# A GLA layer and an S5 layer in one kernel: the S5 kernel products finished a step later, drained by ScalarE, and read as Toeplitz blocks straight from the kernel table

## The chip, the cores and the metric

One core of one Trainium2 chip. The metric is the device time of one execution in microseconds (us); lower is better. Line numbers (L1335) are those of the kernel before, and times from the trace count from the start of its span.

## What is computed

Two layers of a decoder trunk over 512 tokens of width 1024. Layer 0 is chunked gated linear attention (GLA, four heads), layer 1 a state-space mixer (S5) with 128 groups of 16 channels and 64 complex states. Each mixer has a gate path and a residual, and a norm follows. The part that the change touches prepares the S5 layer:

```python
lam_bar = jnp.exp(lam * dt)
b_bar = ((lam_bar - 1.0) / lam)[..., None] * b_cplx
bu = lax.complex(einsum('blgi,gpi->blgp', u32, real(b_bar)),
                 einsum('blgi,gpi->blgp', u32, imag(b_bar)))
_, states = lax.associative_scan(combine, (a, bu), axis=1)
y = einsum('blgp,gip->blgi', real(states), c_re) - einsum('blgp,gip->blgi', imag(states), c_im)
y = gelu(y + d_skip * u32)
y = y * sigmoid(y @ w_glu + b_glu) * silu(z)
```

The kernel does the scan in chunks of T = 8 steps. For each group it needs a 16 x 16 response for every lag within a chunk ("the kernel", C lam_bar^t B, with d_skip at lag 0), laid out as a Toeplitz block of 128 rows (8 steps x 16 channels), and two factors that carry the state in and out of a chunk ("B" and "C" below). All depend on the parameters alone, so they are worked out while layer 0 runs.

## The kernel before, in words

**Layer 0.** For each head, four dense products (proj_v, proj_qk, proj_z, proj_out) run on TensorE (PE). Every factor is split into a high and a low part, and one product is three matmuls (`three`, L201 to L203 or L205 to L207). `wunit` (L176 to L197) brings a weight unit of 512 KB into `wraw` (two buffers) and splits it into two tiles of the ring `whl` (8 tiles before the change). In one form of it ScalarE (ACT) writes the high half (L185) and the negated high half (L186), and a GpSimd (POOL) DMA then adds the weights to the latter in place (L187). In the others VectorE (DVE) or POOL subtracts (L162, L165). Between the products stands the attention itself: scores (L494, L496, masked by DVE L498), their split (L170, L171), the states (L516, L173, L174), and the sum over heads into the residual `xx` (L542).

**The preparation of S5** is the class `S5Prep`, woven into layer 0. There are 16 batches (cb) of 8 groups. `plan` lists steps, and `hook`, called as the dense products advance, takes one whenever a counter that grows by RATES reaches 1. LOWS sets how far a step's priority is lowered, and a step's instructions are held behind the last instruction issued on each engine then. A list scheduler with its own model of durations then fixes the order on every engine. For one batch:

- Step F(cb): `finish_b(cb-1)` adds two halves of the C factor on DVE (`z += z2`, L1325) and stores the B factor to `bmd` (`store`: ACT cast L1319, DVE difference L1320, DMA L1321 on SyncE's queue, SP). `compute(cb)` works on POOL (L1295 to L1313) and leaves bo, z, z2 and bh. `load(cb+1)` issues four loads on SP (L1278, L1280, L1283, L1284). The last, `pp<-pw`, has a single buffer, which `compute` reads at L1304.
- Step Z(cb): `finish_z(cb-1)` stores z to `cmd`, then makes the **kernel product**: four matmuls in fp32 (L1335, eight records each time) of bh and z into one PSUM bank `pt`. ACT drains the even half with a scale (L1339), and DVE reads the odd half from PSUM, scales it and adds the even one in a single instruction (L1341). POOL adds the d_skip term and makes the fp16 pair (L1345 to L1347), and SP stores it to the kernel table `kz` (L1348). Then `gcopy(cb-2)` (L1353) copies, from DRAM to DRAM, the rows of `kz` into full Toeplitz blocks `gmd` (512 KB a batch).

**Layer 1** loads for every batch, by `loadw` (L568 to L584), `bmd`, `tab`, `gmd` and `cmd`, then runs the state products and the scan of the chunks, and after that the w_glu and s_wout products. The loads from `gmd` are six of 256 KB (batches 0 to 2, two each, into `big` tiles) and 13 of 512 KB (into `q` tiles of the ring Q4, 9 tiles).

Of the kernel before, what the change touches and what calls it, by code (L numbers as in the profile page):

```python
# [11 lines left out]
F16 = mybir.dt.float16  # L12
I32 = mybir.dt.int32
U8 = mybir.dt.uint8
AF = mybir.ActivationFunctionType
# [4 lines left out]
MUL, ADD, SUB = ALU.mult, ALU.add, ALU.subtract  # L20

P = 128
# [9 lines left out]
T = 8  # L32
NC = SEQ // T
GB = 8
NB = 16
KW = 15 * 16
# [12 lines left out]
SU = 11  # L49
SS = 22  # L50
SE = 3
WR, WH, Q4, BIG = 2, 8, 9, 28
TOFF = 5
SMALL = [0, 1, 3, 4, 5]
NPRE = 3
# [6 lines left out]
SEQ0 = 'h0 u h2 u h4 u s h6 u x0 t x1 q0 q1 t'  # L62
GP = 4
RATES = [0.84, 0.84, 0.88, 0.94, 0.94]
LOWS = {'F': 0, 'Z': 20, 'E': 100, 'G': 0}
ETABS = [2, 3, 3, 3, 3, 3, 3, 3, 4, 4, 4, 4, 4, 4, 4, 7, 8]
POS = [[0, 0, 1, 2, 1, 2, 3, 1, 2, 3, 3], [0, 1, 1, 3, 4, 5, 6, 5, 5, 7, 9], [0, 1, 3, 4, 4, 5, 6, 5, 6, 8, 8], [1,
    1, 4, 4, 4, 5, 6, 6, 6, 6, 8], [0, 0, 0, 0]]
# [22 lines left out]
def trunk_kernel(  # L91
# [6 lines left out]
    V, A, G, S, PE = nc.vector, nc.scalar, nc.gpsimd, nc.sync, nc.tensor  # L98
    sb = ctx.enter_context(tc.tile_pool(name="sb", bufs=1))
    ps = ctx.enter_context(tc.tile_pool(name="ps", bufs=1, space=PSUM))  # L100
    dr = ctx.enter_context(tc.tile_pool(name="dr", bufs=1, space=DRAM))
    cnt = [0]

    def T_(shape, tag, bufs, dt=F32):
        cnt[0] += 1
        return sb.tile(shape, dt, tag=tag, name=f"{tag}_{cnt[0]}", bufs=bufs)
# [20 lines left out]
    def q4(dt=F32, n=1024):  # L127
        return T_([P, n], "q4", Q4, dt)
# [207 lines left out]
    prep = S5Prep(tc, dr, C_, T_, PT, ident, q4, q2, big, tmp, s_bi, s_xc)  # L336
# [4 lines left out]
    @contextmanager  # L341
    def later(n):
        tc.cur_priority += n
        yield
        tc.cur_priority -= n
# [13 lines left out]
    plan = []  # L359
    ne = 0  # L360
    for cb in range(NB + 1):
# [3 lines left out]
        while ne < ETABS[cb]:  # L365
            plan.append(("E", ne))
            ne += 1
    plan.append(("G", NB - 1))
    pace = [0.0]
    phase = [0]  # L370

    def hook():
        pace[0] += RATES[phase[0]]
        while pace[0] >= 1:
            pace[0] -= 1
            if plan:
                st = plan.pop(0)
                with later(LOWS[st[0]]):
                    prep.step(mark, *st)
# [187 lines left out]

    def loadw(cb, src, dt=F16):  # L568
        n = 1024 if dt == F16 else 512
        if src is prep.gmd:  # L570
            srcs = [src[cb, 4 * k:4 * k + 4].rearrange("g p w -> p g w") for k in range(2)]
            full = src[cb].rearrange("g p w -> p g w")
        else:
            srcs = [src[cb][:, k * n:(k + 1) * n] for k in range(2)]
            full = src[cb]
        fit = (lambda t: t.rearrange("p (g w) -> p g w", w=2 * P)) if src is prep.gmd else (lambda t: t)
        if cb < NPRE:
            w = [T_([P, n], "big", BIG, dt) for _ in range(2)]
            for k in range(2):
                S.dma_start(out=fit(w[k]), in_=srcs[k])  # L580
            return w
        t = q4(dt, 2 * n)
        S.dma_start(out=fit(t), in_=full)
        return [t[:, :n], t[:, n:]]  # L584

    def wsel(w):
        return [[w[k][:, g * P:(g + 1) * P] for g in range(GB)] for k in range(2)]
# [1 line left out]
    def gsel(w):  # L589
        v = [t.rearrange("p (g q k) -> p k g q", k=2, g=GB // 2) for t in w]  # L590
        return [[v[g // 4][:, k, g % 4] for g in range(GB)] for k in range(2)]
# [5 lines left out]

    def load_b(cb):
        t = st_[cb]
        t["gh"] = gsel(loadw(cb, prep.gmd))  # L600
        t["cm"] = wsel(loadw(cb, prep.cmd))

    v0 = ([], [])
# [35 lines left out]
    for h in range(NH):  # L639
# [22 lines left out]
        z = proj_z(h, box)  # L662
# [230 lines left out]
    w = win()  # L893
# [22 lines left out]
    for tb in range(NT):  # L916
        for k in range(2):
            S.dma_start(out=f(x1p)[k * 64:(k + 1) * 64, 2 * tb:2 * tb + 2].rearrange("p q d -> p (q d)"),
                        in_=x1d.rearrange("(c j) d -> j c d", j=T)[2 * tb + k])
# [21 lines left out]
class S5Prep:  # L941
    def __init__(self, tc, dr, C_, T_, PT, ident, q4, q2, big, tmp, s_bi, s_xc):
        self.tc = tc
        self.nc = nc = tc.nc
        self.C_, self.T_, self.PT, self.ident = C_, T_, PT, ident
        self.q4, self.q2, self.big, self.tmp = q4, q2, big, tmp
        self.s_bi, self.s_xc = s_bi, s_xc
        self.kz = dr.tile([NG, 16, KW * 2], F16, name="kz")
        self.bmd = dr.tile([NB, P, 2 * GB * P], F16, name="bmd")
        self.cmd = dr.tile([NB, P, 2 * GB * P], F16, name="cmd")  # L950
        self.gmd = dr.tile([NB, GB, P, 2 * P], F16, name="gmd")
        self.tab = dr.tile([NB, P, 2 * GB * NC], F32, name="tab")
        self.pw = dr.tile([2 * NS, NG, 2 * T], F32, name="pw")
        self.lpt = dr.tile([T, NG, 2, NS], F32, name="lpt")
        self.bcd = dr.tile([2, NS, NG], F32, name="bcd")
        self.r8d = dr.tile([NS, NG], F32, name="r8d")
        self.kdd = dr.tile([NG, 16], F32, name="kdd")
        self.etd = dr.tile([NG], F32, name="etd")
        self.t = 0
        self.ld = {}  # L960
        self.res = {}
# [325 lines left out]
    def compute(self, cb):  # L1287
        G = self.nc.gpsimd
        tt = G.tensor_tensor
        lp, bb, xc, pp = self.ld.pop(cb)  # L1290
        gs = slice(cb * GB, (cb + 1) * GB)
        v = lambda t: t.rearrange("p (g r q) -> p g r q", g=GB, r=2)
        bo, m = self.q4(), self.q4()
        lp4, bb4, bo4, m4 = v(lp), v(bb), v(bo), v(m)
        tt(out=m, in0=lp, in1=bb, op=MUL)  # L1295
        tt(out=bo4[:, :, 0], in0=m4[:, :, 0], in1=m4[:, :, 1], op=SUB)
        tt(out=m4[:, :, 0], in0=lp4[:, :, 0], in1=bb4[:, :, 1], op=MUL)
        tt(out=m4[:, :, 1], in0=lp4[:, :, 1], in1=bb4[:, :, 0], op=MUL)  # L1298
        tt(out=bo4[:, :, 1], in0=m4[:, :, 0], in1=m4[:, :, 1], op=ADD)
        x4 = xc.rearrange("p (g k i) -> p g k i", g=GB, k=4)  # L1300
        z, z2 = self.q4(), m
        sh = [P, GB, T, 16]
        w4 = lambda t: t.rearrange("p (g t i) -> p g t i", g=GB, t=T)
        tt(out=w4(z), in0=x4[:, :, 0].unsqueeze(2).to_broadcast(sh),  # L1304
           in1=pp[:, :, 0:T].unsqueeze(3).to_broadcast(sh), op=MUL)
        tt(out=w4(z2), in0=x4[:, :, 1].unsqueeze(2).to_broadcast(sh),
           in1=pp[:, :, T:].unsqueeze(3).to_broadcast(sh), op=MUL)
        bh = self.C2([P, GB, 16], "bh")
        b2 = self.C2([P, GB, 16], "bh2")
        s3 = [P, GB, 16]  # L1310
        tt(out=bh, in0=x4[:, :, 2], in1=self.BA[:, gs].unsqueeze(2).to_broadcast(s3), op=MUL)
        tt(out=b2, in0=x4[:, :, 3], in1=self.BB[:, gs].unsqueeze(2).to_broadcast(s3), op=MUL)
        tt(out=bh, in0=bh, in1=b2, op=ADD)  # L1313
        self.res[cb] = (bo, z, z2, bh)
# [10 lines left out]
        self.nc.vector.tensor_tensor(out=z, in0=z, in1=z2, op=ADD)  # L1325
        self.store(bo, self.bmd[cb])

    def finish_z(self, cb):
        nc = self.nc
        V, A, PE, S = nc.vector, nc.scalar, nc.tensor, nc.sync  # L1330
        bo, z, z2, bh = self.res.pop(cb)
        self.store(z, self.cmd[cb])
        pk = self.PT()
        for q in range(4):
            PE.matmul(pk[32 * q:32 * q + 32, 0:2 * P],  # L1335
                      lhsT=bh[:, 2 * q:2 * q + 2, :].rearrange("p a b -> p (a b)"),
                      rhs=z[:, 2 * q * P:(2 * q + 2) * P], start=True, stop=True, tile_position=(0, 32 * q))
        ke = self.tmp()[:, :P]
        A.activation(out=ke, in_=pk[:, 0:P], func=AF.Copy, scale=self.par[:, 0:1])  # L1339
        kf = self.C2([P, P, 2], "kf", F16)  # L1340
        V.scalar_tensor_tensor(out=ke, in0=pk[:, P:2 * P], scalar=self.par[:, 1:2], in1=ke, op0=MUL, op1=ADD)  # L1341
        G = nc.gpsimd
        dk = self.C2([P, 16], "dk")
        G.tensor_tensor(out=dk, in0=self.dm, in1=self.kd[:, cb:cb + 1].to_broadcast([P, 16]), op=MUL)
        G.tensor_tensor(out=ke[:, 0:16], in0=ke[:, 0:16], in1=dk, op=ADD)  # L1345
        G.tensor_copy(out=kf[:, :, 0], in_=ke)
        G.tensor_tensor(out=kf[:, :, 1], in0=ke, in1=kf[:, :, 0], op=SUB)  # L1347
        S.dma_start(out=self.kz[cb * GB:(cb + 1) * GB, :, 224:480].rearrange("g i w -> (g i) w"),  # L1348
                    in_=kf.rearrange("p w k -> p (w k)"))

    def gcopy(self, cb):
        src = bass.AP(self.kz.tensor, self.kz[cb * GB].offset + 7 * 32, [[2 * KW, P], [-32, T], [1, 2 * P]])
        self.nc.sync.dma_start(out=self.gmd[cb].rearrange("g (i j) w -> (g i) j w", j=T), in_=src)  # L1353

    def step(self, mark, code, cb):
        with ExitStack() as st:
            for k in ("pe", "act", "dve", "sp"):
                st.enter_context(self.tc.issue_after(mark[k]))
            if code == "F":
                if cb:  # L1360
                    self.finish_b(cb - 1)
                else:
                    self.load(0)
                if cb < NB:
                    self.compute(cb)
                if cb + 1 < NB:
                    self.load(cb + 1)
            elif code == "Z":
                self.finish_z(cb - 1)
                if cb >= 2:  # L1370
                    self.gcopy(cb - 2)
            elif code == "G":
                self.gcopy(cb)
            else:
                self.etab(cb)

# [55 lines left out]
```

## Time and profile before

| | |
|---|---|
| median of 3 runs | 1060.6 us (1058.78 to 1062.19) |
| the profiled execution | 1062.0 us, span 1060.3 us |
| mean granted clock of TensorE | 0.939 of full speed |
| busy time in the span: PE, DVE, POOL, ACT | 935.8, 723.4, 511.7, 465.0 us |
| share of the 16 DMA engines: SP queue, POOL queue | 54.7%, 9.9% |
| read from and written to HBM | 167.7 MB, 45.6 MB |

An engine's busy time is the time in which it worked on an instruction; for PE the ends of matmuls are modelled. The clock column of a view (PEclk) is the share of 2.4 GHz that TensorE was granted. "X <- Y" in a view of waits says that X started when Y ended, by the semaphores in the trace.

### The profile page before, as it was taken

To read this page: it belongs to the slowest core of one execution; us is meant where nothing else is said; L and a number is where in the kernel's file an instruction comes from. 1 tells how busy PE (TensorE), PEld (TensorE's weight loads), DVE (VectorE), ACT (ScalarE), POOL (GpSimd) and SP (SyncE) were. 2 spreads that over 40 slices of the span, in tenths; PEclk is the share of its full clock that TensorE was granted. 3 is DMA by queue.
4 is the path that set the end of the run, shared out by engine and by line. 5 is a ranking of instruction groups with operands and counts; after the bars stand their busy time and mean duration, and the time that the engine had idled before them with its cause. 6 is when DMAs were issued, how large, how long until landed. Compare 5 with 4: busy or idle time off the path is not lost. (4 is left out here: it accounts for less than half of the span.)

```text
span 1060.3 us, 13642 instructions
## 1 busy us (share of the span) xinstructions
PE 935.8 (88%) x5019; PEld 728.6 (69%) x5019; DVE 723.4 (68%) x884; ACT 465.0 (44%) x675; POOL 511.7 (48%) x477
## 2 busy tenths in 40 slices
PE   6895976897779798679979999999998999999996
PEld 5573754575556676557867777777777888888885
DVE  5793569948998889989634778799987432424322
ACT  5553333535445535343545783743453432313222
POOL 4174709877887969898963334353314000000000
PEclk9897987899979898899979999999998999999998
DMA  8884466899779898999578447697864332253312
GB/s 259 225 177 93 88 172 194 249 299 256 224 217 249 223 292 267 238 289 313 197 233 254 142 134 238 200 301 249 266 198 119 113 97 100 93 165 100 100 60 79
DMA packets 118706, 205.78 MB, mean 194 GB/s; under 512 B 32400, under 2 KB 69824, under 8 KB 118640
## 3 DMA queue, kind: packets, MB, share of 16 engines
q1 hardware_dynamic: 110208, 180.90, 54.7%
q0 software_dynamic: 5472, 19.02, 9.9%
q10 hardware_dynamic: 2960, 4.99, 1.3%
q8 instruction: 39, 0.64, 0.2%
q14 instruction: 27, 0.22, 0.1%
HBM read 167.69 MB, written 45.59 MB: 201 GB/s over the span
## 5 line engine op out<-in xcount | busy, mean ns | idle before, releaser
L205 PE MATMUL pd<-whl,actA 128*128 128x512 f32 x384 | 155.7, 414 | 21.6 <-ACT whl L161 9.3
L162 DVE TENSOR_TENSOR whl<-wraw,whl 128x1024 fp32r<-128x1024 f32 x61 | 76.2, 1249 | 144.4 <-ACT whl L161 144.3
L161 ACT CAST whl<-wraw 128x1024 fp32r<-128x1024 f32 x84 | 88.0, 1048 | 166.6 <-PE pt L202 45.7
L206 PE MATMUL pd<-whl,actA 128*128 128x512 f32 x384 | 157.1, 409 | 0.0
L207 PE MATMUL pd<-whl,actA 128*128 128x512 f32 x384 | 156.4, 408 | 0.0
L273 POOL TENSOR_TENSOR rstd<-rv,neghalf 128x1 f32<-128x1 f32 (+1 forms) x6 | 4.3, 716 | 247.1 <-DVE rv L272 247.1
L205 PEld LDWEIGHTS pd<-whl,actA 128*128 128x128 f32 x384 | 75.5, 197 | 42.5 <-ACT whl L161 9.3
L201 PE MATMUL pd<-actA,whl 128*128 128x512 f32 x256 | 101.6, 403 | 3.2 <-ACT u L734 3.2
L203 PE MATMUL pd<-actA,whl 128*128 128x512 f32 x256 | 101.3, 396 | 0.0
L205 PE MATMUL pd<-whl,q 128*128 128x512 f32 x192 | 80.9, 423 | 8.5 <-DVE big L165 3.2
L206 PEld LDWEIGHTS pd<-whl,actA 128*128 128x128 f32 x384 | 75.5, 197 | 17.4 <-issue 1.2
L207 PEld LDWEIGHTS pd<-whl,actA 128*128 128x128 f32 x384 | 75.2, 196 | 17.3 <-issue 1.2
L162 POOL TENSOR_TENSOR whl<-wraw,whl 128x1024 fp32r<-128x1024 f32 x23 | 57.3, 2492 | 52.6 <-ACT whl L161 49.2
L206 PE MATMUL pd<-whl,q 128*128 128x512 f32 x192 | 79.9, 417 | 0.3 <-DVE whl L165 0.3
L1320 DVE TENSOR_TENSOR q<-q,q 128x1024 f16<-128x1024 f32 x32 | 63.7, 1993 | 12.4 <-ACT q L1319 12.4
L1295 POOL TENSOR_TENSOR q<-q,q 128x1024 f32<-128x1024 f32 x16 | 43.5, 2718 | 39.1 <-DMA q<-s_bi 39.1
L201 PEld LDWEIGHTS pd<-actA,whl 128*128 128x128 f32 x256 | 48.4, 189 | 16.3 <-ACT u L734 5.2
L201 PE MATMUL po<-actA,whl 128*128 128x512 f32 x128 | 52.8, 412 | 4.5 <-ACT whl L185 4.5
L203 PEld LDWEIGHTS pd<-actA,whl 128*128 128x128 f32 x256 | 48.4, 189 | 11.3
L1319 ACT CAST q<-q 128x1024 f16<-128x1024 f32 x32 | 33.3, 1042 | 51.3 <-POOL q L1298 15.2
L185 ACT CAST whl<-wraw 128x1024 fp32r<-128x1024 f32 x36 | 37.6, 1046 | 38.3 <-DMA wraw<-w_qk 14.7
L207 PE MATMUL pd<-whl,q 128*128 128x512 f32 x128 | 54.2, 425 | 0.0
(336 smaller groups left out, 2553.1 us busy)
## 6 DMA issues: line engine op xcount, KB each, us to landing
wraw<-w_glu SPq DMA_DIRECT2D x32, 512.0 KB, 3.4
wraw<-w_v SPq DMA_DIRECT2D x16, 512.0 KB, 4.3
wraw<-w_z SPq DMA_DIRECT2D x16, 512.0 KB, 7.0
whl<-w_z POOLq DMA_DIRECT2D x16, 512.0 KB, 8.1
wraw<-w_out SPq DMA_DIRECT2D x16, 512.0 KB, 5.7
q<-lpt SPq DMA_DIRECT2D x16, 512.0 KB, 7.3
q<-s_bi SPq DMA_DIRECT2D x16, 512.0 KB, 8.4
tab<-q SPq DMA_DIRECT2D x32, 256.0 KB, 5.0
```

Source lines behind the costliest of these rows:

```text
L161: i0 = A.copy(out=dst_hi, in_=src)
L162: i1 = E.tensor_tensor(out=dst_lo, in0=src, in1=f(dst_hi), op=SUB)
L185: A.copy(out=hi, in_=raw)
L201: PE.matmul(acc, lhsT=wh, rhs=ah, start=first, stop=False)
L203: mark["pe"] = PE.matmul(acc, lhsT=wl, rhs=ah, start=False, stop=last).ins
L205: PE.matmul(acc, lhsT=ah, rhs=wh, start=first, stop=False)
L206: PE.matmul(acc, lhsT=ah, rhs=wl, start=False, stop=False)
L207: mark["pe"] = PE.matmul(acc, lhsT=al, rhs=wh, start=False, stop=last).ins
L273: G.tensor_tensor(out=dst, in0=v, in1=neghalf.to_broadcast([P, w]), op=ALU.pow)
L1295: tt(out=m, in0=lp, in1=bb, op=MUL)
L1319: nc.scalar.copy(out=hl[:, 0], in_=src)
L1320: nc.vector.tensor_tensor(out=hl[:, 1], in0=src, in1=hl[:, 0], op=SUB)
```

## The change

- The kernel product of a batch leaves step Z and becomes `finish_k`, called at the head of F two steps on (`finish_k(cb-2)` in F(cb)); the last one is a step K. Z keeps the store to `cmd` alone. z and bh of a batch live a step longer: bh gets two buffers, b2 moves to a `tmp` tile, and Q4 grows from 9 to 10 tiles.
- ACT drains both halves of the bank (a second instruction into a second `tmp` tile), and DVE then adds two SBUF tiles.
- `gmd` and `gcopy` go. `load_b` reads each group's Toeplitz block (128 rows of 512 B) from `kz`: eight DMAs of 64 KB a batch, 128 in all, in place of 16 copies and 19 loads.
- To make room, `whl` shrinks from 8 tiles to 7.

```diff
-WR, WH, Q4, BIG = 2, 8, 9, 28
+WR, WH, Q4, BIG = 2, 7, 10, 28
...
-LOWS = {'F': 0, 'Z': 20, 'E': 100, 'G': 0}
+LOWS = {'F': 0, 'Z': 20, 'E': 100, 'K': 20}
...
-    plan.append(("G", NB - 1))
+    plan.append(("K", NB - 1))
...
+        if src is prep.kz:
+            for g in range(GB):
+                S.dma_start(out=w[g // 4][:, g % 4 * 2 * P:(g % 4 + 1) * 2 * P], in_=prep.toep(cb * GB + g))
...
-        t["gh"] = gsel(loadw(cb, prep.gmd))
+        t["gh"] = gsel(loadw(cb, prep.kz))
...
-        bh = self.C2([P, GB, 16], "bh")
-        b2 = self.C2([P, GB, 16], "bh2")
+        bh = self.T_([P, GB, 16], "bh", 2)
+        b2 = self.tmp()[:, :P].rearrange("p (g i) -> p g i", g=GB)
...
-    def finish_z(self, cb):
+    def finish_k(self, cb):
...
         bo, z, z2, bh = self.res.pop(cb)
-        self.store(z, self.cmd[cb])
         pk = self.PT()
...
         ke = self.tmp()[:, :P]
+        ko = self.tmp()[:, :P]
         A.activation(out=ke, in_=pk[:, 0:P], func=AF.Copy, scale=self.par[:, 0:1])
+        A.activation(out=ko, in_=pk[:, P:2 * P], func=AF.Copy, scale=self.par[:, 1:2])
         kf = self.C2([P, P, 2], "kf", F16)
-        V.scalar_tensor_tensor(out=ke, in0=pk[:, P:2 * P], scalar=self.par[:, 1:2], in1=ke, op0=MUL, op1=ADD)
+        V.tensor_tensor(out=ke, in0=ke, in1=ko, op=ADD)
...
-    def gcopy(self, cb):
-        src = bass.AP(self.kz.tensor, self.kz[cb * GB].offset + 7 * 32, [[2 * KW, P], [-32, T], [1, 2 * P]])
-        self.nc.sync.dma_start(out=self.gmd[cb].rearrange("g (i j) w -> (g i) j w", j=T), in_=src)
+    def toep(self, g):
+        return bass.AP(self.kz.tensor, self.kz[g].offset + 7 * 32, [[2 * KW, 16], [-32, T], [1, 2 * P]])
...
             if code == "F":
                 if cb:
+                    if cb > 1:
+                        self.finish_k(cb - 2)
                     self.finish_b(cb - 1)
...
             elif code == "Z":
-                self.finish_z(cb - 1)
-                if cb >= 2:
-                    self.gcopy(cb - 2)
-            elif code == "G":
-                self.gcopy(cb)
+                self.store(self.res[cb - 1][1], self.cmd[cb - 1])
+            elif code == "K":
+                self.finish_k(cb)
```

How this moves instructions, at three places. First DVE around the kernel product of batch 11, in head 3. Before the change (q_653 is z of that batch, the rows of L542 add banks `pd` into the residual, and L1341 drains the product):

```order
L1325 TENSOR_TENSOR q_653_3140<-q_653_3140,q_652_3134 128x1024
L542 TENSOR_TENSOR xx_78<-pd_3323,xx_78 128x512
L542 TENSOR_TENSOR xx_80<-pd_3324,xx_80 128x512
L542 TENSOR_TENSOR xx_82<-pd_3325,xx_82 128x512
L542 TENSOR_TENSOR xx_84<-pd_3326,xx_84 128x512
L1320 TENSOR_TENSOR q_703_3384<-q_653_3140,q_703_3384 128x1024
L1341 SCALAR_TENSOR_TENSOR tmp_3393<-pt_3388,par,tmp_3393 128x128
```

In the changed kernel L1323 is the z add, here that of batch 12 (q_692), and L1340 is the drain of batch 11 (tmp_3448):

```order
L1318 TENSOR_TENSOR q_728_3461<-q_690_3303,q_728_3461 128x1024
L542 TENSOR_TENSOR xx_80<-pd_3335,xx_80 128x512
L1323 TENSOR_TENSOR q_692_3310<-q_692_3310,q_691_3304 128x1024
L542 TENSOR_TENSOR xx_82<-pd_3336,xx_82 128x512
L516 SCALAR_TENSOR_TENSOR big_3435<-po_3431,ges_2674,tmp_3436 128x512
L542 TENSOR_TENSOR xx_84<-pd_3337,xx_84 128x512
L1340 TENSOR_TENSOR tmp_3448<-tmp_3448,tmp_3449 128x128
L173 TENSOR_SCALAR big_3439<-big_3435,ges_2674 128x512
```

The z add that the product of batch 11 needs stood six rows ahead of the drain; it now stands 23 rows ahead, and the add seen here feeds a later product.

Second, SP's queue in head 3, before and after. `kz<-kf` is the store of a kernel, `pp<-pw` the load with a single buffer, `wraw` a weight unit:

```order
L1321 DMA cmd<-q_629_3064 128x2048
L1353 DMA gmd<-kz 1024x1x256
L180 DMA wraw_3484<-w_z 128x1024
L1284 DMA pp_3059<-pw 128x128
L1321 DMA bmd<-q_650_3129 128x2048
L180 DMA wraw_3577<-w_z 128x1024
```

```order
L1319 DMA cmd<-q_714_3395 128x2048
L1347 DMA kz<-kf_3130 128x256
L180 DMA wraw_3700<-w_z 128x1024
L1282 DMA pp_3321<-pw 128x128
L1319 DMA bmd<-q_728_3461 128x2048
L180 DMA wraw_3788<-w_out 128x1024
```

The copy to `gmd` is gone from ahead of the weight load and of `pp`, and the store of a kernel stands in its place.

Third, SP's queue in layer 1, before and after (`yd` is a table of the scan, `s_wz` a weight):

```order
L838 DMA xx_5578<-yd 128x8x64
L583 DMA q_1102_5766<-gmd 128x8x256
L180 DMA wraw_6184<-s_wz 128x1024
L583 DMA q_1103_5768<-cmd 128x2048
L583 DMA q_1128_5987<-bmd 128x2048
L180 DMA wraw_6214<-s_wz 128x1024
```

```order
L577 DMA q_1148_6063<-kz 128x1x256 x8
L180 DMA wraw_6479<-s_wz 128x1024
L582 DMA q_1149_6072<-cmd 128x2048
L582 DMA q_1171_6248<-bmd 128x2048
L837 DMA xx_6029<-yd 128x8x64
L582 DMA q_1172_6250<-tab 128x1024
L180 DMA wraw_6509<-s_wz 128x1024
```

One load of 512 KB became eight of 64 KB in the same place of the queue, ahead of the next weight load.

## Rows read from the trace of the kernel before

**Rows 1.** Busy time by stage: the stretch in us, its length, busy us (and instructions) of PE, PE's weight loads, DVE, ACT and POOL, the granted clock, the share of the DMA engines, and GB/s. The first stretch holds the preparation of the batches beside layer 0, the second the S5 states and scan.

```profile
159.00:556.00 397.00, 329.52 (x1397) 247.22 (x1398) 328.79 (x294) 182.15 (x273) 336.12 (x285) 0.90 0.86 250
556.00:802.00 246.00, 230.66 (x1976) 185.32 (x1976) 200.09 (x243) 135.89 (x189) 94.78 (x65) 0.98 0.69 219
```

**Rows 2.** The same view, the first stretch cut in eight.

```profile
159.00:212.00 53.00, 39.50 (x136) 27.05 (x137) 51.19 (x43) 24.49 (x36) 47.37 (x37) 0.82 0.77 221
212.00:265.00 53.00, 47.08 (x194) 35.08 (x193) 33.84 (x24) 24.36 (x31) 39.47 (x36) 0.95 1.01 277
265.00:318.00 53.00, 40.71 (x166) 29.05 (x166) 50.57 (x58) 23.36 (x39) 46.13 (x39) 0.84 0.73 221
318.00:371.00 53.00, 45.29 (x193) 33.22 (x192) 44.61 (x31) 28.17 (x40) 46.69 (x46) 0.94 0.91 236
371.00:424.00 53.00, 48.33 (x221) 38.05 (x221) 46.81 (x41) 24.98 (x37) 43.59 (x40) 0.94 0.96 279
424.00:477.00 53.00, 37.75 (x165) 28.51 (x164) 50.12 (x42) 20.89 (x35) 45.53 (x39) 0.87 0.92 263
477.00:530.00 53.00, 50.69 (x242) 40.48 (x241) 43.03 (x42) 24.03 (x39) 49.55 (x41) 0.97 0.78 255
530.00:556.00 26.00, 20.18 (x89) 15.78 (x88) 8.62 (x19) 11.87 (x21) 17.79 (x15) 0.79 0.79 239
```

**Rows 3.** Who waited for whom, whole span: engine, tile and line, what it waited for, then us in total, times, longest.

```profile
PE pt L1335 <- DVE q L1325: 20.7, 5, 8.5
PE pt L494 <- DVE tmp L1341: 12.3, 2, 8.0
...
POOL q L1304 <- DMA pp<-pw: 22.4, 5, 7.3
```

**Rows 4.** The timeline around the longest of the five waits of L1335, DVE and PE: start, duration, engine, line, operation; in brackets the idle time before it and what ended it.

```profile
419.76 9.56 DVE L170 CAST big<-att 128x128 fp32r<-128x128 f32 x1
429.35 3.38 DVE L171 TENSOR_TENSOR big<-att,big 128x128 fp32r<-128x128 f32 x1
...
435.96 1.22 DVE L1325 TENSOR_TENSOR q<-q,q 128x1024 f32<-128x1024 f32 x1
437.10 2.47 DVE L542 TENSOR_TENSOR xx<-pd,xx 128x512 f32<-128x512 f32 x4
...
437.23 1.08 PE L1335 MATMUL pt<-q,bh 128*32 128x256 f32 x8 [8.47 <-DVE q L1325]
438.24 0.80 PE L205 MATMUL pd<-whl,actA 128*128 128x512 f32 x1
```

**Rows 5.** The timeline at two other waits of L1335, PE and POOL.

```profile
357.71 1.94 POOL L187 DMA_DIRECT2D whl<-w_qk  x1
...
367.80 1.08 PE L1335 MATMUL pt<-q,bh 128*32 128x256 f32 x8 [5.70 <-DVE q L1325]
...
472.35 0.64 PE L1335 MATMUL pt<-q,bh 128*32 128x256 f32 x8 [4.17 <-DVE q L1325]
475.60 0.79 PE L205 MATMUL pd<-whl,q 128*128 128x512 f32 x1 [2.61 <-DVE tmp L399]
```

**Rows 6.** The timeline at the two waits of L494 for the bank that L1341 empties, DVE and PE.

```profile
295.63 1.75 DVE L165 SCALAR_TENSOR_TENSOR whl<-wraw,hgp,whl 128x512 fp32r<-128x512 f32 x1
...
297.30 0.34 DVE L1341 SCALAR_TENSOR_TENSOR tmp<-pt,par,tmp 128x128 f32<-128x128 f32 x1
...
297.69 0.79 PE L494 MATMUL pt<-big,big 128*128 128x128 f32 x2 [8.05 <-DVE tmp L1341]
...
402.81 0.80 PE L494 MATMUL pt<-big,big 128*128 128x128 f32 x2 [4.21 <-DVE tmp L1341]
```

**Rows 7.** SP's waits (columns as in rows 3) for the copy to `gmd`, and the durations of its issues, min/median/max in ns.

```profile
SPq L1353 <- DMA kz<-kf: 15.6, 6, 5.7
...
L1353 SPq DMA_DIRECT2D gmd<-kz x16: 528/544/750, 218.4 to 561.1; - x16
```

**Rows 8.** Durations of the drain of the product, and beside them of a DVE operation of the same size with two inputs in SBUF. The first two rows are min/median/max in ns, the third is the group of the stretch 159 to 556 (busy us, mean ns, idle before).

```profile
L1341 DVE SCALAR_TENSOR_TENSOR tmp<-pt,par,tmp x16: 333/338/349, 191.7 to 554.6; 128x128 f32<-128x128 f32 x16
L1339 ACT ACTIVATE tmp<-pt,par x16: 345/363/379, 185.8 to 554.1; 128x128 f32<-128x128 f32 x16
...
L171 DVE TENSOR_TENSOR big<-att,big 128x128 fp32r<-128x128 f32 x8 | 12.1, 1507 | 0.2
```

**Rows 9.** What a low half by POOL's DMA costs: ACT's negation, the issue and the landing of the DMA (min/median/max), the POOL operation that can stand ahead of it, and two successive matmuls at full clock.

```profile
L186 ACT ACTIVATE whl<-wraw x36: 1048/1054/1085, 37.8 to 439.2; 128x1024 fp32r<-128x1024 f32 x36
...
L187 POOL DMA_DIRECT2D whl<-w_v x12: 867/890/2527, 87.2 to 386.0; - x12
...
DMA to landing us min/median/max: 5.3/8.1/11.0
...
L1295 POOL TENSOR_TENSOR q<-q,q x16: 2355/2730/3403, 156.7 to 490.2; 128x1024 f32<-128x1024 f32 x16
...
194.61 0.39 PE L205 MATMUL pd<-whl,q 128*128 128x512 f32 x1
194.84 0.39 PE L206 MATMUL pd<-whl,q 128*128 128x512 f32 x1
```

**Rows 10.** SP in the S5 stage: its longest wait from 556 to 802, and the durations of the loads that the change replaces.

```profile
SPq L180 <- POOL whl L162: 59.6, 15, 11.7
...
L583 SPq DMA_DIRECT2D q<-gmd x13: 370/371/433, 574.1 to 782.6; - x13
```

More of the change, by code (lines that the diff above doesn't have):

```diff
@@ L569, in loadw @@
         n = 1024 if dt == F16 else 512
[L570 to L576, printed above, removed]
         if cb < NPRE:
             w = [T_([P, n], "big", BIG, dt) for _ in range(2)]
-            for k in range(2):
[L580 to L584, printed above, removed]
+        else:
+            t = q4(dt, 2 * n)
+            w = [t[:, :n], t[:, n:]]
+        if src is prep.kz:
+            for g in range(GB):
+                S.dma_start(out=w[g // 4][:, g % 4 * 2 * P:(g % 4 + 1) * 2 * P], in_=prep.toep(cb * GB + g))
+        elif cb < NPRE:
+            for k in range(2):
+                S.dma_start(out=w[k], in_=src[cb][:, k * n:(k + 1) * n])
+        else:
+            S.dma_start(out=t, in_=src[cb])
+        return w
     def wsel(w):
@@ L950, in __init__ @@
         self.cmd = dr.tile([NB, P, 2 * GB * P], F16, name="cmd")
-        self.gmd = dr.tile([NB, GB, P, 2 * P], F16, name="gmd")
         self.tab = dr.tile([NB, P, 2 * GB * NC], F32, name="tab")
```

## The prediction

> **What bounds the kernel now.** I read the busy time by stage first [rows 1]. After 556 us PE is busy 94% of the S5 stage, and the preparation that the change edits is over but for the loads. In the first stretch, 159 to 556, nothing is full: PE 329.5 of 397 us, DVE 328.8, POOL 336.1. Cut in eight [rows 2], the busiest engine changes from piece to piece: DVE in three (51.2, 50.6, 50.1 of 53 us), POOL in one (46.7), PE in four. The sum of the busiest of each piece is 364.9, so 397 - 364.9 = 32.1 us is all that could go while each piece keeps its work.
>
> Next, who waited for whom [rows 3]. PE's two largest waits with this preparation are the two that the change aims at: the kernel product waits for the z add, 20.7 us in five places, and the scores L494 wait for the bank that L1341 empties, 12.3 us in two. Together 33.0 us, as much as the slack. POOL waits 22.4 us for `pp`. SP waits 15.6 us for a stored kernel before it can issue the copy [rows 7].
>
> **Part by part.** The sum is made against the profiled execution, 1062.0 us; the median of the runs is 1.4 lower. A measurement of this kernel can tell about 0.3%, 3.2 us, from no change.
>
> (a) *The product a step later.* Its z add now stands 23 DVE rows ahead of the drain instead of six, and one batch of waits goes: 33.0 us nominally, 0 at worst. What is late next, place by place? At the longest, 8.47 us, DVE had been held from 419.76 to 432.7 by L170 and L171 (9.56 and 3.38 us); right behind the z add it empties four banks, 437.10 to 439.57, and PE's next matmul at 438.24 uses one of these [rows 4]. Without L1325 in front, the first L542 comes up to 1.2 us sooner: gain 0 to 1. At 367.80 (5.70 us) the next weights are a `w_qk` unit whose low half left POOL at 359.65; with 8.1 us to land it is there at 367.7 [rows 5, 9]: gain 0 to 2. At 472.35 (4.17 us) the next matmul waits anyway, for L399, another DVE instruction [rows 5]: about 0. The bank wait at 297.69 (8.05 us) follows a DVE that was busy to the end; without the drain the scores' own DVE work is reached about one instruction (0.3 to 1.8 us) sooner [rows 6]: 1.5. The one at 402.81 (4.21 us) may give up to 3.5. With up to 2 for the rest, this reaches 10; I take **-7**. Bounds -32.1 (all, up to the slack) and 0.
>
> (b) *No copy to `gmd`.* Sixteen issues of 0.54 us, 8.7 us of SP, and its 15.6 us of waiting leave the queue [rows 7]. Behind them stood weight loads and `pp`. In the excerpt `pp` still follows a weight load, which waits for its buffer, but no longer the copy; of POOL's 22.4 us of waiting for `pp` [rows 3] some goes, and 8.4 MB less moves in a stretch where the DMA engines are 86% busy [rows 1]. Against it, the store of a kernel, which waits for POOL, now stands in that place. POOL is the busiest engine in one piece of eight only, so its gain reaches the end in part: **-5**, between -22.4 and 0.
>
> (c) *The drain.* ACT gains 16 x 0.36 = 5.8 us [rows 8], hidden: it is busy 182 of 397 us [rows 1]. On DVE an instruction with one PSUM input becomes one with two SBUF inputs. L1341 took 0.333 to 0.349 us all sixteen times. L171, the same size with two SBUF inputs, took 1.51 on average in this stretch while POOL was busy 85% of it [rows 8, 1]. Upper bound: 16 x (1.51 - 0.34) = 18.7 us of DVE; lower bound: nothing, if no drain meets a POOL operation that blocks it. The mean of L171 is its nearest row, and DVE is the busiest engine in three pieces of eight, 159 us of 397: 18.7 x 0.4 = 7.5 at most. Half of these drains should meet no POOL operation that blocks them: **+4**, with bounds 0 and 18.7.
>
> The Trainium skill, "SBUF — State Buffer", section "SBUF: two separate sides", says that VectorE and GpSimd share a port pair under an exclusive lock held for the whole instruction, which a VectorE operation with two SBUF inputs takes against a GpSimd operation that reads SBUF; the loser blocks. This speaks against the new drain, and the constant 0.34 us of L1341 agrees. By the rule alone the drain waits for one POOL operation at most. The trace goes further: L170 held DVE for 9.56 us [rows 4], longer than the longest L1295, 3.40 us [rows 9]. The measurement decides, and the price above is L171's.
>
> (d) *Seven halves.* The ring serves a high and a low half in turn. With eight tiles a low half takes over a low half four units old, so it can start three units ahead of its use; with seven it takes over the high half of three units back, two units ahead. A unit is 24 matmuls of 0.23 us at full clock [rows 9], 5.6 us, so the lead falls from 16.8 to 11.2 us. ACT's negation, POOL's issue and the landing take 1.05 + 0.89 + 8.1 = 10.0 [rows 9]: it just fits, unless a POOL operation of 2.7 us (L1295) stands ahead, which makes 12.8, short by 1.6. In the stretch 24 units go this way. If half met such an operation: 12 x 1.6 = 19. But PE was slower than full clock, and waited elsewhere, in most pieces (granted 0.82 to 0.97 [rows 2]), which lengthens the lead. I take **+1.5**, bounds 0 and 19.
>
> (e) *128 loads in place of 35 issues.* 93 more at 0.37 us are 34 us of SP [rows 10], nearly all in the S5 stage. There SP's longest wait alone, for a weight buffer that POOL is reading, is 59.6 us; it covers them. The blocks come in the same 512 B rows. If weight loads behind a burst of eight (3 us) come late, 13 bursts x 1 us = 13. I take **+1**, bounds 0 and 13.
>
> The extra lifetime of z costs no time as long as Q4's tenth tile carries it. b2 and the odd half use `tmp` tiles, four of them; both are freed within a step, and I price it at nothing; if POOL's reads free them late, ACT waits, which has 215 us to spare.
>
> Sum: -7 - 5 + 4 + 1.5 + 1 = -5.5, 1056.5 by the profiled execution, and 1.4 lower, **1055.0**, by the median.
>
> **The rivals.**
>
> *Bigger gain.* The waits in (a) vanish nearly in full because DVE's order no longer puts the z add, the drain and PE in one chain. For it: 33.0 us of PE's waiting hangs on this chain and 32.1 us of slack is there [rows 2, 3]. Against it: the place-by-place reading above. With -27 for (a) and (c) to (e) as taken and (b) within the slack, 1062.0 - 27 - 5 + 6.5 = 1036.5, 1035 by the median.
>
> *No change.* DVE, held up by POOL, is the real bound where PE waits; the waits pass to L542, L399, L498. Then (a) is -2, (b) -3, (c) to (e) +4: 1061, 1059.6 by the median. For it: in three of the five places read the next wait is on DVE too.
>
> *Slower by the halves.* The ring of seven is the mechanism: PE waits at the low half of a unit (L206 or L203) for POOL's DMA. It decides once POOL's queue ahead of L187 exceeds 11.2 - 10.0, about 1.2 us, in more than five or so of the 24 units of the stretch: with all of it, 1062.0 - 7 (the other four terms) + 19 = 1074.0, 1072.6 by the median. For it: POOL is 85% busy, and one L187 took 2.53 us to issue [rows 9]. Against it: PE's clock and other waits lengthen the lead.
>
> *Slower by the drain.* Each L1340 is blocked as L171 was: +18.7 on DVE, all of it where DVE is late, and (a) gains nothing: 1062 + 18.7 - 5 - 7 = about 1069, 1067 by the median. For it: L171's mean, and its one of 3.38 us [rows 4, 8]. Against it: a mean of 1.51 over eight leaves room for several that met nothing. By the section of the Trainium skill named above, every drain that starts under a POOL operation is blocked; no run so far shows this for L1340.
>
> *Slower by the bursts.* (e) at its bound with (a) small: 1065.
>
> **How the numbers follow.** The small gain, own range 1048 to 1057.4, 0.36; the bigger gain 0.14; no change 0.18; the halves 0.16; the drain 0.10; the bursts 0.06. Faster by over 0.3%: 0.36 + 0.14 = 0.50; within it 0.18; slower 0.16 + 0.10 + 0.06 = 0.32. The predicted time is that of the likeliest, 1055.0. The range takes in the bigger gain almost to its point (1036) and the halves to 1073; what lies outside is the rest of these two, under 0.2.
>
> **What would show it.** Right: in the profile after, no wait of the product's matmuls for the z add and none of L494 for the drain, while PE's waits for L542 or L399 have grown; POOL's wait for `pp` under 15 us; L1340 between 0.3 and 1.5 us in the mean; SP's waits in the S5 stage down by some 30 us at an unchanged length of 246. Wrong: PE waiting for POOL's L187 at low halves by 10 us or more; L1340 above 1.5 us; the S5 stage longer; or the stretch to the end of the preparation shorter by 15 us or more.

## The result, and the profile after

The changed kernel takes 1074.99 us (median of 4 runs, 1072.17 to 1078.10), the kernel before 1061.39 in the same comparison: ratio 1.0124, 95% interval 1.0086 to 1.0163. The forecast was 1055, range 1036 to 1073. The profiled execution took 1078.1 us, span 1076.4, clock 0.932. Ratios here and below leave disturbed runs out, so one can differ a little from the quotient of two medians.

Busy time of the two stages, columns as in [rows 1]:

```profile
159.00:556.00 397.00, 321.76 (x1374) 242.82 (x1375) 301.10 (x292) 178.13 (x276) 325.32 (x277) 0.88 0.79 224
556.00:802.00 246.00, 227.55 (x1906) 181.89 (x1905) 194.73 (x246) 136.05 (x192) 85.59 (x61) 0.97 0.66 209
```

In the first stretch PE, DVE and POOL all did less than before, and the DMA engines were less busy (0.79 against 0.86); in a slower kernel part of this work falls behind 556 us. Nothing has become a fuller engine (over the whole span PE is busy 933.8 us and DVE 701.4, before 935.8 and 723.4); all of them wait more. To see where, I lined up the matmuls of L201 to L207 of both traces in order of time. The 450th starts 20.0 us later than before (161.4 us there), the 1425th only 3.9 later (501.5), the 1575th 16.0 (539.7), the 1650th 9.5 (573.7), the 1800th 15.2 (621.4); from there the lag lies mostly between 13 and 18 and ends at 15.9. So by this count most of the loss made early in layer 0 is made up again; what is kept arises around the seam to layer 1 and in the first part of the S5 stage, and the last products add nothing.

Who waited for whom, the rows that answer to [rows 3], and PE's largest waits:

```profile
PE pd L205 <- ACT whl L161: 15.4, 2, 10.2
PE pt L494 <- DVE big L162: 14.8, 2, 13.9
PE pd L205 <- DVE big L165: 13.6, 3, 8.8
PE po L205 <- ACT big L164: 10.3, 2, 5.2
PE pd L206 <- DMA whl<-w_z: 9.6, 3, 5.5
PE pd L205 <- DVE tmp L399: 9.5, 1, 9.5
...
POOL q L1302 <- DMA pp<-pw: 6.8, 2, 6.1
...
PE pt L494 <- ACT tmp L1338: 2.3, 1, 2.3
...
PE pd L206 <- DMA whl<-w_v: 0.9, 1, 0.9
```

What was aimed at is gone: no wait of the product for the z add is left, the scores wait 2.3 us for the drain instead of 12.3, POOL 6.8 us for `pp` instead of 22.4. In their place stand waits for halves of weights (L161, and POOL's DMA into `whl`) and for attention work on ACT and DVE.

The waits of ACT and DVE when they split a weight unit show the source (the high half is written in L161, L164 or L185, the low half in L162 or, first, in L186). Before:

```profile
DVE whl L162 <- ACT whl L161: 144.3, 45, 5.8
...
ACT whl L161 <- PE pt L202: 45.7, 12, 4.6
...
ACT whl L164 <- DMA wraw<-w_out: 14.9, 2, 9.3
ACT whl L161 <- DMA wraw<-s_wu: 14.8, 4, 8.7
...
ACT whl L185 <- DMA wraw<-w_z: 10.6, 5, 3.7
...
ACT whl L161 <- DMA wraw<-w_glu: 7.3, 1, 7.3
```

After:

```profile
ACT whl L164 <- DMA wraw<-w_out: 43.5, 10, 10.3
DVE whl L162 <- PE pt L202: 38.3, 10, 4.4
...
ACT whl L161 <- PE pt L203: 37.3, 10, 4.6
DVE whl L162 <- PE pd L202: 31.3, 9, 4.4
...
ACT whl L161 <- DMA wraw<-s_wu: 27.0, 8, 13.1
...
ACT whl L185 <- DMA wraw<-w_z: 23.4, 8, 9.3
...
ACT whl L161 <- DMA wraw<-w_glu: 19.8, 7, 8.1
...
ACT whl L186 <- PE pd L206: 16.4, 10, 3.7
```

In the code L202 is the last reader of a high half and L203 the reader of a low one. With eight tiles the two halves of a unit take over the two halves of the unit four back: ACT's L161 waits for L202, and DVE's L162, which writes the low half, then waits for ACT alone. With seven the low half takes over the high half of the unit three back, which is read one unit later: now L162 itself waits for L202, and in the other form ACT's second copy (L186) waits for PE. These writers of the low half are the last readers of the raw buffer. There are two raw buffers, so each comes free later and the load two units on is issued later. Summed over all weights, ACT's waits for raw weights go from 74.0 to 159.4 us.

How such a wait reaches PE is seen in the timeline at the 450th matmul. Before, ACT:

```profile
149.85 0.27 ACT L161 CAST big<-pt 128x128 fp32r<-128x128 f32 x1 [0.78 <-DVE att L498]
...
160.02 1.33 ACT L164 ACTIVATE whl<-wraw,hgp 128x512 fp32r<-128x512 f32 x2 [9.31 <-DMA wraw<-w_out]
```

After, ACT, DVE and PE:

```profile
155.27 1.33 ACT L164 ACTIVATE whl<-wraw,hgp 128x512 fp32r<-128x512 f32 x2 [10.35 <-DMA wraw<-w_out]
...
156.02 1.46 DVE L165 SCALAR_TENSOR_TENSOR whl<-wraw,hgp,whl 128x512 fp32r<-128x512 f32 x1 [6.04 <-ACT whl L164]
...
156.51 0.24 ACT L161 CAST big<-pt 128x128 fp32r<-128x128 f32 x1
...
161.07 0.28 DVE L162 TENSOR_TENSOR big<-pt,big 128x128 fp32r<-128x128 f32 x1
...
161.40 0.79 PE L494 MATMUL pt<-big,big 128*128 128x128 f32 x2 [13.91 <-DVE big L162]
```

The wait for `w_out` is about as long in both. Before, it stood behind ACT's three copies of the transposed keys out of the bank of the scores (L161, 128x128); after, the order puts it in front of two of them. ACT holds 10.35 us, DVE behind it, and PE 13.9 us behind both. At 541.92 the same happens at the seam: ACT waits 13.06 us for a `s_wu` unit, and PE 5.2. Neither wait is the whole loss: of the lag of 20.0 us at the 450th matmul 3.9 are left at the 1425th.

### The profile page after: what moved, and what is told of

Read it like the earlier page. It is cut to its first block, busy times and chain, and to the rows that moved or that the text cites. A ratio compares the mean times of both kernels' runs of the same rounds, so it can differ in the third digit from the quotient of the medians.

```text
span 1076.4 us, 13775 instructions
## 1 busy us (share of the span) xinstructions
PE 933.8 (87%) x5019; PEld 728.6 (68%) x5019; DVE 701.4 (65%) x884; ACT 469.7 (44%) x691; POOL 504.8 (47%) x477
## 5 line engine op out<-in xcount | busy, mean ns | idle before, releaser
L205 PE MATMUL pd<-whl,actA 128*128 128x512 f32 x384 | 157.0, 420 | 25.5 <-ACT whl L161 15.4
L162 DVE TENSOR_TENSOR whl<-wraw,whl 128x1024 fp32r<-128x1024 f32 x61 | 78.0, 1278 | 149.7 <-PE pt L202 38.3
L161 ACT CAST whl<-wraw 128x1024 fp32r<-128x1024 f32 x84 | 88.1, 1049 | 188.6 <-PE pt L203 37.3
L206 PE MATMUL pd<-whl,actA 128*128 128x512 f32 x384 | 160.5, 418 | 11.0 <-DMA whl<-w_z 9.6
L207 PE MATMUL pd<-whl,actA 128*128 128x512 f32 x384 | 159.5, 417 | 0.0
L205 PEld LDWEIGHTS pd<-whl,actA 128*128 128x128 f32 x384 | 76.6, 200 | 46.2 <-ACT whl L161 15.8
L201 PE MATMUL pd<-actA,whl 128*128 128x512 f32 x256 | 102.2, 406 | 2.8 <-ACT u L733 2.6
L203 PE MATMUL pd<-actA,whl 128*128 128x512 f32 x256 | 101.8, 400 | 0.0
L205 PE MATMUL pd<-whl,q 128*128 128x512 f32 x192 | 80.7, 420 | 23.3 <-DVE big L165 13.6
L206 PEld LDWEIGHTS pd<-whl,actA 128*128 128x128 f32 x384 | 77.6, 202 | 31.3 <-DMA whl<-w_z 9.7
L207 PEld LDWEIGHTS pd<-whl,actA 128*128 128x128 f32 x384 | 77.8, 203 | 18.9 <-issue 1.8
L206 PE MATMUL pd<-whl,q 128*128 128x512 f32 x192 | 78.7, 411 | 0.0
L162 POOL TENSOR_TENSOR whl<-wraw,whl 128x1024 fp32r<-128x1024 f32 x23 | 57.7, 2511 | 35.4 <-ACT whl L161 10.4
L205 PEld LDWEIGHTS pd<-whl,q 128*128 128x128 f32 x192 | 37.7, 197 | 36.4 <-DVE big L165 15.4
L185 ACT CAST whl<-wraw 128x1024 fp32r<-128x1024 f32 x36 | 37.5, 1043 | 50.9 <-DMA wraw<-w_z 23.4
L201 PEld LDWEIGHTS pd<-actA,whl 128*128 128x128 f32 x256 | 48.9, 191 | 15.0 <-ACT u L733 3.5
L201 PE MATMUL po<-actA,whl 128*128 128x512 f32 x128 | 52.0, 406 | 7.7 <-ACT big L530 4.2
L203 PEld LDWEIGHTS pd<-actA,whl 128*128 128x128 f32 x256 | 48.9, 191 | 11.7
L207 PE MATMUL pd<-whl,q 128*128 128x512 f32 x128 | 52.4, 414 | 0.0
```

Source lines behind the costliest of these rows:

```text
L161: i0 = A.copy(out=dst_hi, in_=src)
L162: i1 = E.tensor_tensor(out=dst_lo, in0=src, in1=f(dst_hi), op=SUB)
L185: A.copy(out=hi, in_=raw)
L201: PE.matmul(acc, lhsT=wh, rhs=ah, start=first, stop=False)
L203: mark["pe"] = PE.matmul(acc, lhsT=wl, rhs=ah, start=False, stop=last).ins
L205: PE.matmul(acc, lhsT=ah, rhs=wh, start=first, stop=False)
```

## Experiments

Each was compared with the kernel before on the same chip. The theories: **halves** (the ring of seven tiles costs; "the seventh tile" below means the step from eight tiles to seven), **drain** (ACT's drain and a DVE add that POOL blocks), **late product** (z held longer), and later **order** (the scheduler's order changes with every edit, and orders differ in time).

**Undo the seventh tile, or do it alone.** Changed kernel, and kernel before:

```diff
-WR, WH, Q4, BIG = 2, 7, 10, 28
+WR, WH, Q4, BIG = 2, 8, 9, 28      # e1, in the changed kernel
-WR, WH, Q4, BIG = 2, 8, 9, 28
+WR, WH, Q4, BIG = 2, 7, 10, 28     # e2, in the kernel before
```

> The changed kernel with the ring of halves back at 8 tiles and Q4 back at 9 (same memory); later product, ACT drain and direct Toeplitz reads stay. Halves theory: the 13.5 us of loss come from the seventh tile, so the time falls to 1061 or below (1055 if the other parts gain what was forecast), and the waits of ACT's split for raw weights (w_out 43.5, w_z 23.4 us in the changed kernel) fall back to about 15 and 11 us. Drain theory and late-product theory: still 1070 to 1080, the waits for raw weights may fall all the same.

> The kernel before with 7 halves and Q4 at 10, nothing else changed. Halves theory: slower by 10 to 16 us, 1071 to 1077, with PE waiting for a low half (DMA into whl) by some 10 us and ACT's split waiting for raw weights by 30 us or more in w_out. Drain and late-product theories: within 3 us of 1061.

Eight halves: 1072.20, ratio 1.0130 (1.0098 to 1.0163), raw waits 79.0 us: no gain, against the halves theory. Seven alone: 1069.74, 1.0110 (1.0074 to 1.0147), raw waits 138.8: for it. Both cannot be the whole story.

**Undo the drain, or do it alone** (`ko`, the second ACT copy and the DVE add out of the changed kernel, or into the one before).

> The changed kernel with the old drain: ACT takes the even half, DVE scales and adds the odd half straight from PSUM; later product, direct reads and 7 halves stay. Drain theory: DVE no longer waits 15 us for ACT's second half nor is blocked by POOL, 1060 to 1066. Halves and late-product theories: 1072 to 1078.

> The kernel before with the new drain alone (ACT takes both halves, DVE adds two SBUF tiles); the product, the copy and 8 halves as before. Drain theory: slower by 5 to 15 us, 1066 to 1076, with the add on DVE above 1 us in the mean. Halves and late-product theories: within 3 us of 1061, the add at 0.3 to 0.8 us.

Without it: 1072.75, 1.0151 (1.0109 to 1.0193). Alone: 1060.53, 1.0013 (0.9989 to 1.0038). The drain alone is not the cause. On DVE it does cost; the groups of the add, in the changed kernel and with the drain alone:

```profile
L1340 DVE TENSOR_TENSOR tmp<-tmp,tmp 128x128 f32<-128x128 f32 x16 | 15.5, 969 | 15.1 <-ACT tmp L1338 15.1
```

```profile
L1343 DVE TENSOR_TENSOR tmp<-tmp,tmp 128x128 f32<-128x128 f32 x16 | 19.5, 1217 | 7.5 <-ACT tmp L1341 7.5
```

Means of 0.97 and 1.22 us against 0.34 [rows 8], 10 to 14 us of DVE time that the total does not show.

**The other parts alone, and no part at all.** Direct reads alone (e5: `gmd`, `gcopy` and step G out, `toep` in); the later product alone (e6: `finish_k` in F and last in G, old drain and copy kept); and RATES alone, lower (e7) and higher (e8):

```diff
-RATES = [0.84, 0.84, 0.88, 0.94, 0.94]
+RATES = [0.82, 0.82, 0.86, 0.92, 0.92]     # e7
+RATES = [0.86, 0.86, 0.90, 0.96, 0.96]     # e8
```

> The kernel before with the direct Toeplitz reads alone: no copy to gmd, eight loads of 64 KB a batch from kz; product, drain, 8 halves and Q4 at 9 as before. Theory that the reads are harmless and the missing copy helps: 1053 to 1060, POOL's wait for pp below 15 us (20 to 22 with the copy). Theory that the bursts of loads delay weights in the S5 stage: 1064 to 1072, with the loss after 556 us and ACT's split waiting longer for s_wu and s_wz weights. Theory that a changed order alone costs (the order before was fitted to its step list): 1063 to 1072 with the loss in the stretch 150 to 556.

> The kernel before with the product a step later alone: old drain, copy kept, 8 halves, Q4 at 9, so that z lives a step longer in the same 9 tiles. Late-product theory (z and bh held longer, Q4 short): 1068 to 1076, with POOL's L1295 waiting for q tiles or for DMAs that free them. If the later product is harmless and only the halves and the reads cost: 1053 to 1062, with PE's 33 us of waits at the product gone.

> The kernel before with all RATES lowered by 0.02: no work changes, each step of the preparation comes a little later. Theory that the order was fitted and any shift of steps costs: 1064 to 1075, with new PE waits near 160 us. Theory that losses need a mechanism (halves, q tiles, reads): within 3 us of 1059.

> The kernel before with all RATES raised by 0.02, each step a little earlier. Fitted-order theory: 1064 to 1075. Mechanism theory: within 3 us of 1059.

Direct reads: 1066.56, 1.0088 (1.0059 to 1.0116). Later product: 1058.87, 0.9971 (0.9940 to 1.0002), but against the expectation PE still waits 17.8 us in three places for the z add. Rates lower: 1062.14, 1.0043 (1.0019 to 1.0068); higher: 1076.71, 1.0181 (1.0141 to 1.0220). The last is the most telling: with no work changed, the order alone costs up to 1.8%, more than the change. A loss of 1% in one order proves nothing about a part; it has to be seen in another.

**Double the tile, and a second order.** Six halves in the kernel before (f1, WH 6, Q4 9); in the lowered rates the changed kernel (f2) and the direct reads (f3); and later product and drain together (f4) in the first order.

> The kernel before with a ring of 6 halves (Q4 at 9, two tiles of memory left empty), nothing else changed: doubles the suspected cost of the seventh tile. Halves theory: a unit's high half can then be split only when the unit three back is done, the lead falls by another unit, ACT's waits for raw weights go from 74 us (8 halves) and 139 us (7) to 200 or more, and the time to 1090 or more, well outside what a changed order has done (1062 and 1077 with the rates moved). Order theory: 1060 to 1077 like any other order, raw-weight waits as with 7.

> The changed kernel, 7 halves, with all RATES lowered by 0.02, as in the run of the kernel before that gave 1062. Halves theory: the waits for raw weights stay at 140 to 160 us and the time at 1068 to 1080 in this order too. Order theory: the loss is that of one order, and this one may fall anywhere between 1055 and 1075.

> Direct Toeplitz reads alone, 8 halves, RATES lowered by 0.02. If the loss of 0.9% with direct reads was that of an order and not of the reads: 1054 to 1064, within 3 us of the 1062 that the lowered rates gave with the copy. If the reads cost in themselves: 1068 to 1073.

> The kernel before with the later product and the ACT drain together; copy kept, 8 halves, Q4 at 9. Each alone gave a ratio of 0.997 and 1.001. If the halves and the missing copy's order carry the loss: 1054 to 1062. If the later product and the drain hurt each other (DVE's add waits for ACT's second half, 15 us in the changed kernel): 1066 to 1074.

Six halves: 1074.09, 1.0141 (1.0094 to 1.0188), not 1090, and raw waits of 61.9 us: the expectation failed. Both halves now wait for PE before ACT gets to look at the raw buffer, so the wait moves in the table (ACT's splits wait 194.1 us for PE, against 158.6), and the cost does not grow with each tile. Changed kernel: 1075.33, 1.0188 (1.0135 to 1.0241), raw waits 136.6. Direct reads: 1058.50, 1.0006 (0.9976 to 1.0035), so their 0.9% was an order's. Later product and drain: 1066.09, 1.0094 (1.0060 to 1.0128).

**The parts in the second order** (RATES as in e7):

> Seven halves alone (Q4 at 10), RATES lowered by 0.02. If the seventh tile costs in itself: raw-weight waits near 140 us again and 1068 to 1078. If 1.011 was that of an order: 1056 to 1066.

> The later product alone, 8 halves, copy kept, old drain, RATES lowered by 0.02. If the later product is neutral to helpful in itself: 1052 to 1064, near the 1062 of the kernel before in this order. If 0.997 was a lucky order: 1066 to 1076.

> Later product and ACT drain, 8 halves, copy kept, RATES lowered by 0.02. If the 1.009 of these two in the first order was an order's: 1054 to 1064. If the two hurt each other: 1066 to 1076.

> The changed kernel with 8 halves and Q4 at 9, RATES lowered by 0.02. With 7 halves this order gave a ratio of 1.019. If the seventh tile is what costs: 1056 to 1066 here. If the other parts cost in themselves: 1068 to 1078 again, as 1.013 in the first order.

| ratio to the kernel before | first order | rates lower |
|---|---|---|
| kernel before | 1 | 1.0043 |
| seven halves alone | 1.0110 | 1.0143 (1.0108 to 1.0179) |
| later product alone | 0.9971 | 1.0027 (1.0002 to 1.0052) |
| later product and drain | 1.0094 | 0.9957 (0.9929 to 0.9984) |
| direct reads alone | 1.0088 | 1.0006 |
| changed kernel, eight halves | 1.0130 | 0.9983 (0.9962 to 1.0004) |
| changed kernel | 1.0124 | 1.0188 |

With eight halves every part comes level with the kernel before or below it in at least one order. Only seven halves with two raw buffers lose in both orders tried, alone and in the changed kernel, 1.1 to 1.9%. Eight halves in the changed kernel recover 2 points in the second order and none in the first. All these runs with seven halves have Q4 at 10; the two were not taken apart, but six halves with Q4 at 9 lose as well.

**Which chain of the seventh tile.** A third raw buffer in the memory of one Q4 tile, in the kernel before (h1) and the changed one (h2), rates lower:

```diff
-WR, WH, Q4, BIG = 2, 7, 10, 28
+WR, WH, Q4, BIG = 3, 7, 9, 28
```

> The kernel before, RATES lowered by 0.02, 7 halves, three raw buffers, Q4 at 9 (the memory of the kernel before). Late raw weights as the chain: ACT's waits for raw weights fall from 135 us to 75 or less and the time from 1074 to 1058 to 1064. Lead of the low halves as the chain: the raw waits fall all the same, ACT's L186 still waits for PE by 15 us or more and POOL's L187 for ACT by 35 or more, and the time stays at 1069 to 1079.

> The changed kernel, RATES lowered by 0.02, 7 halves, three raw buffers, Q4 at 9. With two raw buffers and Q4 at 10 this order gave a ratio of 1.019, with 8 halves 0.998. Late raw weights as the chain: 0.998 to 1.006. Lead of the low halves as the chain: 1.012 to 1.022.

1046.72, 0.9877 (0.9846 to 0.9907), and 1050.00, 0.9897 (0.9854 to 0.9941). This is for late raw weights as the chain, with both faster than that theory expected. Seven halves with two raw buffers (g1):

```profile
POOL whl L187 <- ACT whl L186: 37.7, 12, 8.8
...
ACT whl L185 <- DMA wraw<-w_z: 24.6, 6, 15.0
...
ACT whl L164 <- DMA wraw<-w_out: 20.7, 8, 7.0
...
ACT whl L186 <- PE pd L206: 15.6, 9, 3.9
```

With three (h1):

```profile
POOL whl L187 <- ACT whl L186: 34.9, 11, 12.1
...
ACT whl L186 <- PE pd L206: 22.1, 6, 5.1
...
ACT whl L186 <- PE po L202: 19.5, 4, 9.2
...
ACT whl L164 <- DMA wraw<-w_out: 17.6, 3, 9.2
```

ACT's second copy still waits for PE, longer than in g1, and POOL's DMA for it about as long; of the waits of the split those for raw weights fell, from 135.0 to 33.0 us in all (`w_z` has no row left), and the time is 27.6 us below that of g1. PE's waits for a low half's DMA did not fall (5.0 us in g1, 7.1 in h1). So it is not the lead of the low halves that costs most. The kernel before has 74 us of waits for raw weights as well, which fits that these two versions beat it: h1 is the fastest kernel of the study, 1.2% below the kernel before. Both runs are in one order, and Q4 goes back to 9 with the third buffer. A third raw buffer with eight halves, which takes one tile more, was not tried.

Two readings of these traces limit the account. First, h1 has the wait at the place of the 450th matmul too, longer than the changed kernel:

```profile
160.79 0.80 PE L494 MATMUL pt<-big,big 128*128 128x128 f32 x2 [17.96 <-DVE big L162]
```

So this wait shows how a late weight reaches PE, and not where the loss lies. Second, from the 1650th to the 2400th matmul, 242.0 us in the kernel before, all seven traces with seven halves take 246.9 to 248.4 us, those with three raw buffers too; eleven of the twelve with eight take 237.9 to 244.7, and the later product alone 248.7. Some 6 us of the cost of seven halves seem to fall there, and the third raw buffer does not give them back; which wait makes them was not traced.

## Why the prediction was wrong

The sum failed at two steps. The first is **(d), seven halves**: taken as +1.5, it measured +1.1% alone in the first order (about 12 us) and 1.0 point over the same order with eight (1.0143 against 1.0043). The bounds, 0 and 19, held it, and the rival of the halves gave 1072.6 for a measured 1075.0. But its mechanism was only in part what was named. PE's waits for POOL's low-half DMA are there, 10.5 us with the row of `w_v`, which crosses the mark that the prediction set; but the drain alone, with eight halves, has 6.9 us of them (`w_qk`) and loses nothing. The larger part is one step upstream: a low half that is written later frees the raw buffer later. I worked out the lead of the halves tile by tile and never asked who waits for the split to finish: SP, with the next load of 512 KB. (24 matmuls of 0.23 us are 5.5 us, not 5.6, so the two leads are 16.6 and 11.0; by that the upper bound is about 21.) Another sign of being wrong came too: the S5 stage is longer, by 6.4 us from the 1650th to the 2400th matmul.

The second is a term that the sum did not have, the order (last point below): with eight halves back the changed kernel still lost 1.3% in the order measured, and nothing in the second. Either would account for the loss alone, so how its 13.6 us divide between the two stays open. That the time came out near the halves' rival is in part luck.

- **(a) The product a step later, -7.** In the changed kernel PE's waits at the product fell from 25.0 us (20.7 for the z add and 4.3 for a bank) to 6.5. But the later product alone still has 17.8 us for the z add in the first order, and seven halves alone, with the product where it was, has 1.5: how long these waits are depends on the whole order. The later product alone gave 0.9971 and 1.0027 (in an order at 1.0043), about -3 and -2 us, neither clear of noise. The place-by-place reading, which let most of the 33 us pass to the next wait, was right in kind and still too generous; the bigger gain was rightly doubted.
- **(b) No copy, -5, and (e) the loads, +1.** POOL's wait for `pp` fell under 15 us as forecast and bought nothing: direct reads gave 1.0088 and 1.0006. Nor was the copy its reason: with the copy kept, RATES alone took it from 22.4 to 11.0 us (e7). The loads alone cost no time: with direct reads alone the lag is 6.0 us at the 1650th matmul and 3.6 at the end, although one issue took 0.60 us in the changed kernel, not 0.37:

```profile
L577 SPq DMA_DIRECT2D q<-kz x104: 514/597/2109, 588.7 to 797.3; - x104
```

- **(c) The drain, +4.** DVE paid 10 to 14 us, inside the bounds of 0 and 18.7 and between the 0.3 and 1.5 us set for one; alone the end paid 1.4 us (interval -1.2 to 4.0). By the rule of the Trainium skill, "SBUF — State Buffer", section "SBUF: two separate sides", an add with two SBUF inputs is blocked by a GpSimd operation that reads SBUF and started first, and the trace agrees: in the changed kernel the five drains that met no POOL instruction took 0.28 to 0.29 us, and most of the others ended about 0.15 us after the POOL instruction under which they had started. That its price at the end was nothing fits DVE not being the bound where it fell; this was not shown. On top of the later product it cost 1.2 points in the first order and gained 0.7 in the second.
- **What no term had: the order.** Every edit passes through a scheduler that places instructions by its own durations, and an order can put a wait for weights ahead of attention work on ACT, for 10 us or more of PE at one place, though not always at the end. RATES alone moved the time by 0.4 and 1.8%. A range that ended at 1073 for terms of 5 us was too narrow by this alone.

Not settled: why eight halves in the changed kernel lose 1.3% in the first order and nothing in the second, and likewise later product and drain. An order's cost fits both: e1 has, at the 450th matmul, the wait for `w_out` ahead of the split of the values, and PE waits 12.8 us there. But so has the later product alone (10.4 us), and it lost nothing in the end. Which waits of those orders last to the end was not shown.

## What to carry to other kernels

Before a buffer is taken from a ring to pay for something else, follow its release upstream: here the missing tile held up less its reader than the load two units ahead, and in the one order tried the same memory as a third raw buffer, and not as a tenth Q4 tile, was worth 2.7 points. In a kernel whose order a scheduler sets, price an edit in two orders at least (shift a rate, measure the unchanged kernel too); a loss or gain of 1% in one order is not yet the edit's. A wait that vanishes from the list is a gain only if nothing behind it waits as long.

## What the runs showed of the hardware

A DVE add of 128 x 128 with two SBUF inputs took 0.275 us at best, 0.97 and 1.22 in the mean and up to 6.95 beside a busy POOL (drain alone), up to 9.22 in the run of later product and drain; the form with one PSUM input kept to 0.33 to 0.35. The longest POOL instruction of these two runs took 3.38 and 4.15 us, so more than one POOL operation can hold such an add. Issuing a 64 KB read of 512 B rows that overlap in DRAM took 0.60 us on SP in the median, a 512 KB load of plain blocks 0.37 [rows 10].
